# A two-layer decoder trunk on TensorE: x held at another address outside the feed-forward layers, four pairs of sums moved from GpSimd to VectorE, and two wide products ahead of four streams of narrow ones

## The chip, the cores and the metric

The kernel runs on one core of a Trainium2 chip. The metric is the device time of one execution in microseconds (us), and a figure for a kernel is the median of several runs. The engines are named as the profile names them: PE is TensorE (PEld its weight loads), DVE is VectorE, ACT is ScalarE, POOL is GpSimd, SP issues the DMAs.

## The reference

Input and output are 512 tokens of 1024 channels in float32. Layer 0 has native sparse attention (nsa) as its mixer, layer 1 a gated linear recurrence (hgrn); each mixer stands between two feed-forward layers (FFNs) of inner width 2816.

```python
def _swiglu(x, w_gate, w_up, w_down):
    return (jax.nn.silu(x @ w_gate) * (x @ w_up)) @ w_down

    for i in range(DEPTH):                      # DEPTH = 2
        x = _layer_norm(alpha * x + 0.5 * _swiglu(x, ffn1_w_gate[i], ffn1_w_up[i], ffn1_w_down[i]),
                        ln_gain[i, 0], ln_bias[i, 0])
        ...
        y = _nsa(x, ...) if kind == 0 else _hgrn2(x, ...)
        x = _layer_norm(alpha * x + y, ln_gain[i, 1], ln_bias[i, 1])
        x = _layer_norm(alpha * x + 0.5 * _swiglu(x, ffn2_w_gate[i], ffn2_w_up[i], ffn2_w_down[i]),
                        ln_gain[i, 2], ln_bias[i, 2])
```

Both mixers begin with a projection `x @ w_in` and end with one by `w_out`.

## The kernel before

Every float32 operand of a large product is split into a high part (`whi`, `xh`, `xhi`), written by ACT (`split`, L112), and the rest (`wlo`, `xl`, `xlo`), written by DVE (L113). A product is then three products of PE (`mm3`, L128 to L130): high by high, and each high part by the other's rest. In a row such as `ps<-xh,whi` the output stands ahead of the arrow, then the operand that streams through PE (moving), then the one that PEld loads (stationary).

The stages follow one another: FFN 1, nsa, FFN 2 of layer 0, then FFN 1, hgrn, FFN 2 of layer 1. In the profiled execution they begin at about 5, 355, 707, 1051, 1398 and 1745 us. The four FFNs are one function, `ffn_body`. It works on the inner width in two halves, of 12 and 10 blocks of 128, and a group `g` is two such blocks for gate and up together. Group 0 is done by `plain_pair` with products of 256 columns. Every other group is done by `seven`: seven products of half-size blocks (24 PE products of 256 columns each) in place of eight, with sums and differences of the weights formed on DVE (L350, `form`) and of the results on DVE as well (`q2` at L402, `q3` at L404, then L408 to L415). Product 4 of a call that is not `seeded` (groups 1 and 2) needs `q3`. The second half of each FFN consists of five such calls, 840 products. Behind each half stands `down`, products of 512 columns (`ps<-whi,xhi` and its two fellows).

The transposed x is held as `xh` and `xl` in the pool `xt`. In `plain_pair` of group 0, x comes in four blocks of 128 tokens. For blocks 0 and 1 their parts are summed back to float32 (`xb`, L272, a slice of `h`), two instructions of 128 x 1024 on POOL; for blocks 2 and 3 `token_forms` (L173 to L177, DVE) makes the differences between token halves from them, from which the tiles `t0h` to `t2l` are split. Ahead of this stands the layer norm of the stage before (`ln_tok`): statistics and L200, L215, L216 on DVE, and three small POOL instructions L204, L189, L190 between the statistics and L216.

The bytes modulo 256 at which an operand begins in a partition: in the FFNs 224 for `xh`, `xl` and the tiles t0h to t2l, 32 for `whi`, `wlo`, and 32 for both operands of `down`. In the mixers' projections x is at 224 and the weights are at 32, in 96 products at 0. In the mixers x is the moving operand for keys and queries (`ps<-xh,whi`, 480 of them 512 columns wide) and the stationary one where the result has tokens on the partitions (`ps<-whi,xh`, 672 of them 512 wide with weights at 32); 288 more of both kinds are 256 columns wide.

The order on PE is that of the program. On DVE, ACT, POOL and SP a scheduler chooses the order by its own estimates of when each instruction could begin, so that an instruction given to another engine can change the order of its neighbours.

## Time and profile before

| | |
|---|---|
| median of 3 runs | 2110.07 us (2104.12, 2110.07, 2110.17) |
| the profiled execution, and its span | 2099.54 us, 2097.8 us |
| busy: PE, PEld, DVE, ACT, POOL | 98%, 90%, 68%, 47%, 10% |
| mean granted clock of PE | 0.995 |

The profile is of one execution, some 10 us below the median of the runs. Its times within the span are those of the trace. A product's duration in it is modelled; what a stream of products costs is read from the starts, as the distance from one start to the next, which is called the pace here.

### The profile page before, as it was taken

The page shows a single profiled execution, that of the slowest core. Times are in us where ns is not written, and L with a number is a line of the kernel's source. Part 1 is how long each engine was busy: PE and PEld are TensorE (multiplying, and loading weights), DVE is VectorE, ACT ScalarE, POOL GpSimd, SP SyncE. Part 2 cuts the span into 40 slices and gives each one's busy share as a digit, 9 for nine tenths or more (in the row PEclk, how much of TensorE's full clock was granted, in tenths as well). Part 3 has the DMA queues.
Part 4 walks back from the last instruction along what each step waited for, and adds up shares of the span by engine and source line. Part 5 has one row for each costly group of instructions (what it writes and reads, how often), then busy time and mean ns, then how long its engine had stood idle before and what let it go on. Part 6 is the DMA issues. An engine that isn't in the chain of part 4 may idle for free.

```text
span 2097.8 us, 34590 instructions
## 1 busy us (share of the span) xinstructions
PE 2055.2 (98%) x14277; PEld 1885.4 (90%) x14277; DVE 1418.3 (68%) x2124; ACT 976.1 (47%) x1570; POOL 217.2 (10%) x321
## 2 busy tenths in 40 slices
PE   8999999999999999999999999999999999999998
PEld 8998998879898899899899989988788989998996
DVE  8946855377775896486598467664636858955864
ACT  5543552255565354255345335435536734543551
POOL 1000002001122300000110000021321213000002
PEclk9999999999999999999999999999999999999999
DMA  5441342231011145133234412512231023342331
GB/s 181 122 150 51 102 145 76 82 110 41 31 31 51 61 125 157 48 113 115 67 121 124 138 57 86 172 60 90 82 116 31 2 71 101 115 147 61 101 121 41
DMA packets 138762, 194.00 MB, mean 92 GB/s; under 512 B 8571, under 2 KB 117435, under 8 KB 138604
## 3 DMA queue, kind: packets, MB, share of 16 engines
q1 hardware_dynamic: 138604, 191.79, 29.6%
q8 instruction: 112, 1.84, 0.4%
q14 instruction: 46, 0.38, 0.1%
HBM read 189.58 MB, written 2.19 MB: 91 GB/s over the span
## 4 chain that ended last, share of the span: by engine, by line
PE 83%; DVE 10%; POOL 2%; ACT 2%; issue 1%; DMA 1%; DVEq 0%; POOLq 0%; SPq 0%; ACTq 0%
PE ps L128 23%; PE ps L130 23%; PE ps L129 23%; PE po L820 3%; DVE wlo L113 2%; PE ps L804 2%; PE ps L1148 1%; DVE raw L350 1%; PE sc L771 1%; PE sc L772 1%; DVE st L201 1%; DVE x L200 1%; PE ps L543 1%; DVE xl L113 1%; ACT whi L112 1%
## 5 line engine op out<-in xcount | busy, mean ns | idle before, releaser
L113 DVE TENSOR_TENSOR wlo<-raw,whi 128x1024 fp32r<-128x1024 f32 (+1 forms) x253 | 315.2, 1250 | 275.0 <-ACT whi L112 274.3
L112 ACT ACTIVATE whi<-raw 128x1024 fp32r<-128x1024 f32 (+1 forms) x253 | 265.6, 1055 | 359.7 <-PE ps L130 164.5
L128 PE MATMUL ps<-xh,whi 128*128 128x256 f32 (+1 forms) x1120 | 332.9, 297 | 3.0 <-ACT whi L112 1.6
L130 PE MATMUL ps<-xh,wlo 128*128 128x256 f32 (+1 forms) x1120 | 331.1, 296 | 2.3 <-DVE wlo L113 2.3
L129 PE MATMUL ps<-xl,whi 128*128 128x256 f32 (+1 forms) x1120 | 331.0, 296 | 1.2 <-DVE xl L113 1.2
L130 PE MATMUL ps<-whi,xlo 128*128 128x512 f32 x704 | 274.4, 390 | 1.5 <-DVE xlo L113 1.5
L128 PE MATMUL ps<-whi,xhi 128*128 128x512 f32 x704 | 274.4, 390 | 0.0
L129 PE MATMUL ps<-wlo,xhi 128*128 128x512 f32 x704 | 274.0, 389 | 0.0
L130 PEld LDWEIGHTS ps<-xh,wlo 128*128 128x128 f32 x1120 | 212.3, 190 | 10.2 <-DVE wlo L113 2.8
L128 PEld LDWEIGHTS ps<-xh,whi 128*128 128x128 f32 x1120 | 210.8, 188 | 11.8 <-ACT whi L112 2.0
L129 PEld LDWEIGHTS ps<-xl,whi 128*128 128x128 f32 x1120 | 211.0, 188 | 8.9 <-DVE xl L113 1.8
L128 PE MATMUL ps<-xh,xhi 128*128 128x256 f32 x640 | 180.2, 282 | 7.3 <-DVE q L404 7.2
L112 ACT ACTIVATE whi<-fr 128x1024 fp32r<-128x1024 f32 x120 | 126.7, 1059 | 118.6 <-PE ps L129 83.8
L129 PE MATMUL ps<-xl,xhi 128*128 128x256 f32 x640 | 179.8, 281 | 0.0
L130 PE MATMUL ps<-xh,xlo 128*128 128x256 f32 x640 | 179.8, 281 | 0.0
L113 DVE TENSOR_TENSOR wlo<-fr,whi 128x1024 fp32r<-128x1024 f32 x120 | 146.8, 1224 | 47.4 <-ACT whi L112 47.1
L130 PEld LDWEIGHTS ps<-whi,xlo 128*128 128x128 f32 x704 | 132.2, 188 | 30.7 <-DVE xlo L113 3.2
L129 PEld LDWEIGHTS ps<-wlo,xhi 128*128 128x128 f32 x704 | 132.2, 188 | 26.8
L128 PEld LDWEIGHTS ps<-whi,xhi 128*128 128x128 f32 x704 | 132.2, 188 | 26.8
L350 DVE TENSOR_TENSOR raw<-fr 128x1024 f32<-128x1024 f32 x120 | 145.8, 1220 | 13.1 <-DMA fr<-in_ffn_w_up_dram 11.4
L113 DVE TENSOR_TENSOR xlo<-h,xhi 128x1024 fp32r<-128x1024 f32 x44 | 53.9, 1226 | 111.8 <-ACT xhi L112 111.8
L128 PEld LDWEIGHTS ps<-xh,xhi 128*128 128x128 f32 x640 | 121.6, 190 | 8.1 <-DVE q L404 7.8
(267 smaller groups left out, 4737.7 us busy)
## 6 DMA issues: line engine op xcount, KB each, us to landing
raw<-in_ffn_w_down_dram SPq DMA_DIRECT2D x88, 512.0 KB, 3.5
fr<-in_ffn_w_gate_dram SPq DMA_DIRECT2D x80, 512.0 KB, 4.0
fr<-in_ffn_w_up_dram SPq DMA_DIRECT2D x80, 512.0 KB, 5.0
raw<-in_hgrn_w_in_dram SPq DMA_DIRECT2D x32, 512.0 KB, 4.2
raw<-in_nsa_w_in_dram SPq DMA_DIRECT2D x18, 512.0 KB, 3.9
raw<-in_ffn_w_gate_dram SPq DMA_DIRECT2D x8, 512.0 KB, 5.4
raw<-in_ffn_w_up_dram SPq DMA_DIRECT2D x8, 512.0 KB, 4.5
raw<-in_nsa_w_out_dram SPq DMA_DIRECT2D x8, 512.0 KB, 3.4
```

Source lines behind the costliest of these rows:

```text
L112: a = self.nc.scalar.activation(hi, src, AF.Copy)
L113: b = self.nc.vector.tensor_tensor(lo, src, hi.bitcast(F32), op=ALU.subtract)
L128: mm(out, l[0], r[0], start=start, stop=False)
L129: mm(out, l[0], r[1], start=False, stop=False)
L130: mm(out, l[1], r[0], start=False, stop=stop)
L200: nc.vector.scalar_tensor_tensor(x[:, s], x[:, s], float(scale), banks[h], op0=ALU.mult, op1=ALU.add)
L201: nc.vector.bn_stats(st[:, h, :], x[:, s])
L350: tt(out, x, y, op=op)
L543: nc.tensor.matmul(ph, w1[:, j, :], self.ap(z[:, 0:1], 2 * j, [[16, 129]]), start=j == 0, stop=j == 15)
L771: nc.tensor.matmul(sc[:, t - ts[0], :], l, kh[t][g][:, :n], start=True, stop=False)
L804: nc.tensor.transpose(p[:, j * P : j * P + P], pf[:, (b0 + j) * P : (b0 + j + 1) * P], self.ident)
L820: nc.tensor.matmul(po[:, ii, t, :], pt[:, t * (i + 1) + j, :], v[j][:, t, g, :], start=j == 0, stop=j == i)
```

## The change

The tiles of `xh` and `xl` become 64 bytes longer, and `place_xt` sets where x begins in them: at 0 (224 modulo 256, as before) or at 64 bytes (32 modulo 256). In `finish` of the first FFN of each layer x goes to 64 before the first new block is written, in `finish` of the mixer back to 0. So x is at 32 modulo 256 throughout nsa and hgrn, and at 224 in the FFNs. `out_proj` of nsa takes its views of the old x (`ox`) before that. The sums L272 are given to DVE in place of POOL. In the first call of `seven` in an FFN's second half two products of 512 columns, `xh` by `whi`, are put ahead of product 1; their result is overwritten and used by nobody.

```diff
+PLACE = 64
@@ new_xt
-        self.xh = pool.tile([P, 2, NK, 2 * P], F32R, name="xh")
-        self.xl = pool.tile([P, 2, NK, 2 * P], F32R, name="xl")
+        self.xbuf = [pool.tile([P, NK * T + 64], F32R, name=n) for n in ("xh", "xl")]
+        self.place_xt(0)
+
+    def place_xt(self, n):
+        self.xh, self.xl = (b[:, n // 4 : n // 4 + NK * T].rearrange("p (a k t) -> p a k t", a=2, k=NK) for b in self.xbuf)
@@ finish
                 if h == 0 and c >= 2:
+                    self.place_xt(self.place)
                     self.flush(c - 2)
@@ ffn_body
-                                nc.gpsimd.tensor_tensor(xb[:, k], self.xh[:, 0, ks].bitcast(F32), self.xl[:, 0, ks].bitcast(F32), op=ALU.add)
+                                nc.vector.tensor_tensor(xb[:, k], self.xh[:, 0, ks].bitcast(F32), self.xl[:, 0, ks].bitcast(F32), op=ALU.add)
...
-                        self.seven(mid, tf, w3, g, h[:, 2 * pr : 2 * pr + 2, :], g >= NSTD + 2)
+                        self.seven(mid, tf, w3, g, h[:, 2 * pr : 2 * pr + 2, :], g >= NSTD + 2, half == 1 and pr == 0)
@@ seven
+        if first:
+            for _ in range(2):
+                nc.tensor.matmul(b, w[1][0][:, 0, 0, :], self.xr(0)[0], start=True, stop=True, skip_group_check=True)
         product(1, a, True)
@@ out_proj
+        if xh is None:
+            ox = [self.xc(k, c) for k in range(NK) for c in range(NT)]
...
-                l = self.xc(k, c) if xh is None else (xh[k][:, c * P : c * P + P], xl[k][:, c * P : c * P + P])
+                l = ox[NT * k + c] if xh is None else (xh[k][:, c * P : c * P + P], xl[k][:, c * P : c * P + P])
@@ body
-    for r, t.nxt in zip(run, first[1:] + [None]):
+    for r, t.nxt, t.place in zip(run, first[1:] + [None], (PLACE, 0, 0, PLACE, 0, 0)):
```

The change moves instructions on PE, DVE, POOL and, a little, ACT; SP's order of loads is the same in both kernels. The new file has its lines 7 to 12 further down (L113 becomes L120, L200 L207, L204 L211, L216 L223, L272 L280, L330 L338, L350 L358, L402 L414, L404 L416).

The first place is PE's passage from `down` to the second half of an FFN, here the first one. Before:

```order
L128 MATMUL ps<-whi,xhi 128x512
L129 MATMUL ps<-wlo,xhi 128x512
L130 MATMUL ps<-whi,xlo 128x512
L128 MATMUL ps<-xh,whi 128x256
L129 MATMUL ps<-xl,whi 128x256
L130 MATMUL ps<-xh,wlo 128x256
```

In the changed kernel the same passage reads:

```order
L135 MATMUL ps<-whi,xhi 128x512
L136 MATMUL ps<-wlo,xhi 128x512
L137 MATMUL ps<-whi,xlo 128x512
L404 MATMUL ps<-xh,whi 128x512 x2
L135 MATMUL ps<-xh,whi 128x256
L136 MATMUL ps<-xl,whi 128x256
L137 MATMUL ps<-xh,wlo 128x256
```

The two products stand between the last wide product of `down` and the first narrow one; on PE nothing else has moved anywhere.

The second place is the head of FFN 1 of layer 1, where the layer norm of token block 3 (x_74) meets the sums. DVE before, from the splits of blocks ahead to the second step of the norm:

```order
L113 TENSOR_TENSOR xl<-ps,xh 128x4x128 x2
L201 BN_STATS st<-x_74 128x6
L200 SCALAR_TENSOR_TENSOR x_74<-x_74,ps 128x512
L201 BN_STATS st<-x_74 128x6
L202 BN_AGGR mv<-st 128x2
L215 SCALAR_TENSOR_TENSOR x_74<-x_74,mv,lng 128x512 x2
L216 SCALAR_TENSOR_TENSOR x_74<-x_74,ry,lnb 128x512 x2
```

POOL before, at the same place:

```order
L212 TENSOR_TENSOR x_73<-x_73,lng 128x512
L213 TENSOR_TENSOR x_73<-x_73,lnb 128x512
L272 TENSOR_TENSOR h<-xh,xl 128x1024 x2
L204 TENSOR_SCALAR lm<-mv 128x1
L189 TENSOR_SCALAR ry<-mv 128x1
L190 TENSOR_TENSOR ry<-ry,mhalf 128x1
```

DVE in the changed kernel:

```order
L120 TENSOR_TENSOR xl<-ps,xh 128x4x128 x2
L208 BN_STATS st<-x_74 128x6
L207 SCALAR_TENSOR_TENSOR x_74<-x_74,ps 128x512
L280 TENSOR_TENSOR h<-xh,xl 128x1024
L208 BN_STATS st<-x_74 128x6
L280 TENSOR_TENSOR h<-xh,xl 128x1024
L209 BN_AGGR mv<-st 128x2
L222 SCALAR_TENSOR_TENSOR x_74<-x_74,mv,lng 128x512 x2
L223 SCALAR_TENSOR_TENSOR x_74<-x_74,ry,lnb 128x512 x2
```

The two sums stand ahead of the norm's statistics `mv` on DVE now, and on POOL nothing stands any more between L220 (before: L213) and L211 (before: L204). In FFN 2 of both layers the two L280 rows stand right behind the two L223 rows of block 3, ahead of the split `xl` of block 2; in the first FFN of all they stand behind the first three splits `wlo<-raw,whi`.

The third place is DVE's way to `q3` of group 1, here in FFN 2 of layer 0. Before:

```order
L113 TENSOR_TENSOR wlo<-fr,whi 128x1024
L113 TENSOR_TENSOR xlo<-raw,xhi 128x1024
L330 TENSOR_TENSOR h<-ps,sg 128x512
L113 TENSOR_TENSOR xl<-h,xh 128x1024
L113 TENSOR_TENSOR wlo<-fr,whi 128x1024
L113 TENSOR_TENSOR wlo<-raw,whi 128x1024
L113 TENSOR_TENSOR wlo<-fr,whi 128x1024
L350 TENSOR_TENSOR raw<-fr 128x1024 x2
L113 TENSOR_TENSOR wlo<-raw,whi 128x1024
L402 TENSOR_TENSOR q_7785<-ps,p_7784 128x512
L350 TENSOR_TENSOR fr<-fr,raw 128x8x128
L404 TENSOR_TENSOR q_7865<-ps,q_7785 128x512
```

In the changed kernel:

```order
L120 TENSOR_TENSOR wlo<-fr,whi 128x1024
L338 TENSOR_TENSOR h<-ps,sg 128x512
L120 TENSOR_TENSOR xl<-h,xh 128x1024
L120 TENSOR_TENSOR wlo<-fr,whi 128x1024
L120 TENSOR_TENSOR wlo<-raw,whi 128x1024
L358 TENSOR_TENSOR raw<-fr 128x1024
L120 TENSOR_TENSOR wlo<-fr,whi 128x1024
L358 TENSOR_TENSOR raw<-fr 128x1024
L120 TENSOR_TENSOR xlo<-raw,xhi 128x1024
L414 TENSOR_TENSOR q_7787<-ps,p_7786 128x512
L120 TENSOR_TENSOR wlo<-raw,whi 128x1024
L416 TENSOR_TENSOR q_7867<-ps,q_7787 128x512
```

Counted from the first L173 (now L180) of block 2, 20 instructions of 128 x 1024 elements stand ahead of L404 before, and 18 ahead of L416 now: one `form` raw<-fr and the `form` fr<-fr,raw have moved behind it. The same holds for the FFNs of layer 1.

## Rows read from the trace of the kernel before

**Rows 1.** The page: the span, the busy time of each engine with its share of the span and its instructions, and the chain that ended last, by engine.

```profile
span 2097.8 us, 34590 instructions
...
PE 2055.2 (98%) x14277; PEld 1885.4 (90%) x14277; DVE 1418.3 (68%) x2124; ACT 976.1 (47%) x1570; POOL 217.2 (10%) x321
...
PE 83%; DVE 10%; POOL 2%; ACT 2%; issue 1%; DMA 1%; DVEq 0%; POOLq 0%; SPq 0%; ACTq 0%
```

**Rows 2.** The timeline of PE in the first FFN: start, duration, engine, line, operation and tiles. The first and the last of 91 rows in its first half, then the first and the last of 87 rows in its second half.

```profile
59.78 0.28 PE L129 MATMUL ps<-t2l,whi 128*128 128x256 f32 x1
...
69.98 0.28 PE L129 MATMUL ps<-t0l,whi 128*128 128x256 f32 x1
...
249.76 0.28 PE L129 MATMUL ps<-xl,whi 128*128 128x256 f32 x1
...
259.89 0.28 PE L128 MATMUL ps<-xh,whi 128*128 128x256 f32 x1
```

**Rows 3.** Busy time by windows, PE alone: the window, its length, busy us (and products), granted clock, share and GB/s of the DMA engines. The first row lies in the first half of FFN 1 of layer 0, the next to last in that of FFN 2 of layer 1; the others lie in the second halves of the four FFNs. Products that run over a window's edge count in it.

```profile
83.00:133.00 50.00, 50.00 (x443) 1.00 0.54 164
...
245.00:295.00 50.00, 50.00 (x427) 1.00 0.31 95
...
900.00:950.00 50.00, 50.00 (x427) 1.00 0.33 97
...
1245.00:1295.00 50.00, 50.00 (x427) 1.00 0.29 90
1800.00:1850.00 50.00, 50.00 (x443) 1.00 0.39 121
1940.00:1990.00 50.00, 50.00 (x427) 1.00 0.34 104
```

**Rows 4.** The timeline of PE, streams of 512 columns: the first and the last of 46 rows of `down`, of 46 rows of hgrn with x stationary, and of 45 rows of hgrn with x moving.

```profile
159.68 0.39 PE L128 MATMUL ps<-whi,xhi 128*128 128x512 f32 x1
...
169.88 0.39 PE L128 MATMUL ps<-whi,xhi 128*128 128x512 f32 x1
...
1519.68 0.39 PE L130 MATMUL ps<-whi,xl 128*128 128x512 f32 x1
...
1529.98 0.39 PE L130 MATMUL ps<-whi,xl 128*128 128x512 f32 x1
...
1559.62 0.39 PE L129 MATMUL ps<-xl,whi 128*128 128x512 f32 x1
...
1569.89 0.39 PE L128 MATMUL ps<-xh,whi 128*128 128x512 f32 x1
```

**Rows 5.** The timeline of PE at two passages into streams of 256 columns: from `down` into the second half of the first FFN, and behind a wait of PE at the head of FFN 2 of layer 0. In brackets: idle time ahead of the row and what ended it.

```profile
198.89 0.39 PE L130 MATMUL ps<-whi,xlo 128*128 128x512 f32 x1
199.12 0.28 PE L128 MATMUL ps<-xh,whi 128*128 128x256 f32 x1
199.24 0.28 PE L129 MATMUL ps<-xl,whi 128*128 128x256 f32 x1
...
720.68 0.39 PE L129 MATMUL ps<-xl,whi 128*128 128x256 f32 x1 [0.48 <-DVE xl L113]
720.90 0.28 PE L130 MATMUL ps<-xh,wlo 128*128 128x256 f32 x1
```

**Rows 6.** The timelines of POOL and DVE at the heads of three FFNs: first FFN, FFN 2 of layer 0, FFN 1 of layer 1.

```profile
8.84 5.68 POOL L272 TENSOR_TENSOR h<-xh,xl 128x1024 f32<-128x1024 f32 x2 [7.55 <-DVE xl L113]
...
9.87 6.87 DVE L113 TENSOR_TENSOR wlo<-raw,whi 128x1024 fp32r<-128x1024 f32 x3 [0.25 <-ACT whi L112]
...
712.99 4.75 POOL L272 TENSOR_TENSOR h<-xh,xl 128x1024 f32<-128x1024 f32 x2 [1.62 <-DVE x L216]
...
715.41 0.69 DVE L173 TENSOR_TENSOR h<-ps,h 128x512 f32<-128x512 f32 x1 [1.99 <-POOL h L272]
...
1052.62 5.21 POOL L272 TENSOR_TENSOR h<-xh,xl 128x1024 f32<-128x1024 f32 x2
1057.81 0.66 POOL L204 TENSOR_SCALAR lm<-mv 128x1 f32<-128x1 f32 x1
...
1053.95 4.44 DVE L215 SCALAR_TENSOR_TENSOR x<-x,mv,lng 128x512 f32<-128x512 f32 x2
1059.33 1.41 DVE L216 SCALAR_TENSOR_TENSOR x<-x,ry,lnb 128x512 f32<-128x512 f32 x2 [0.95 <-POOL ry L190]
```

**Rows 7.** The timelines of PE and DVE at the waits of PE near the heads of the FFNs: first FFN, FFN 2 of layer 0, FFN 1 of layer 1 (three rows of PE and DVE, and its wait for the norm), FFN 2 of layer 1.

```profile
12.34 0.58 PE L130 MATMUL ps<-xh,wlo 128*128 128x256 f32 x1 [1.96 <-DVE wlo L113]
...
747.84 0.38 PE L128 MATMUL ps<-xh,xhi 128*128 128x256 f32 x1 [2.50 <-DVE q L404]
...
1060.14 0.55 PE L159 MATMUL ps<-ident,x 128*128 128x128 f32 x3 [1.60 <-DVE x L216]
...
1091.60 1.22 DVE L350 TENSOR_TENSOR fr<-fr,raw 128x1024 f32<-128x1024 f32 x1
1092.73 0.68 DVE L404 TENSOR_TENSOR q<-ps,q 128x512 f32<-128x512 f32 x1
...
1093.47 0.39 PE L128 MATMUL ps<-xh,xhi 128*128 128x256 f32 x1 [2.00 <-DVE q L404]
...
1786.52 0.39 PE L128 MATMUL ps<-xh,xhi 128*128 128x256 f32 x1 [2.69 <-DVE q L404]
```

**Rows 8.** Busy time by windows behind the waits for L404: the window, its length, then busy us (and instructions) of PE, PEld, DVE, ACT and POOL, granted clock, share and GB/s of the DMA engines.

```profile
1091.40:1098.40 7.00, 5.00 (x30) 4.93 (x30) 7.00 (x9) 3.36 (x4) 0.00 (x0) 0.76 0.16 34
...
1786.60:1793.60 7.00, 7.00 (x48) 7.00 (x49) 7.00 (x9) 4.01 (x5) 0.00 (x0) 0.76 0.49 146
...
747.00:754.00 7.00, 6.06 (x50) 5.86 (x51) 7.00 (x10) 4.14 (x5) 0.00 (x0) 1.00 0.33 99
```

More of the change, by code (lines that the diff above doesn't have):

```diff
@@ L330, in plain_pair, with seven @@
             nc.vector.tensor_tensor(h[:, fc, :], banks[2 + fc], sg, op=ALU.mult)
-    def seven(self, pool, tf, w3, g, h, seeded):
+    def seven(self, pool, tf, w3, g, h, seeded, first):
         nc = self.nc
```

## The prediction

> **What bounds the kernel now.** I read the page first: PE is busy for 2055 of 2098 us and carries 83% of the chain that ended last, DVE 10%, POOL 2% [rows 1]. So the time is PE's products times their pace, plus some 40 us in which it is idle; only what changes a pace or a wait of PE counts. A "busy" PE is no PE at its best, however, so next I read starts. Products of 256 columns run at two paces: (69.98 - 59.78) / 90 = 113.3 ns in the first half of the first FFN, (259.89 - 249.76) / 86 = 117.8 ns in its second [rows 2], with the same operands at the same addresses. The windows tell that this is no accident of one place: 443 products fit in 50 us of first halves, 427 in 50 us of each of the four second halves, with the granted clock at 1.00 in all [rows 3]. Products of 512 columns have a pace that goes with the address: 10.20 / 45 = 226.7 ns in `down` (both operands at 32 modulo 256), 10.30 / 45 = 228.9 with x stationary at 224, 10.27 / 44 = 233.4 with x moving at 224 [rows 4]. Last I read who ends PE's waits at the heads of the FFNs: DVE, in every row [rows 7], and there DVE itself had been held by POOL [rows 6].
>
> **Part 1, x at 32 in the mixers.** The 480 wide products with x moving get both operands at 32, as in `down`: 480 x (233.4 - 226.7) = 3.2 us less. The 672 with x stationary: 672 x (228.9 - 226.7) = 1.5 us. For the 96 with weights at 0 and for those of 256 and fewer columns no row has the new pair of addresses; the nearest are the two paces of [rows 2], so 288 products of 256 columns move by 0 to 4.5 ns either way, up to 1.3 us. I take 0 there. A little of this may be lost where attention is waiting for something else: I take -4.6 us, between 0 and -6. `place_xt` and `ox` are only views; the three orders of the mixers are as before, so they cost nothing.
>
> **Part 2, the sums on DVE.** On POOL a pair took 5.68, 4.75 and 5.21 us [rows 6]. On DVE an instruction of this size stands 1092.73 - 1091.60 = 1.13 us ahead of the next [rows 7], so a pair adds 2.3 us to DVE's queue. What hides it: DVE sat 1.99 us waiting for POOL's sums at 715.41, and beside them its own work was slow: three `wlo` took 6.87 us where 3.5 is three of 1.13 and a tail, two L215 took 4.44 where the two L216 took 1.41 [rows 6]. Without that cover it would be 2.3 us later for all that is queued behind it, the splits `xl` of block 2 and the token forms first. Head by head:
>
> First FFN: PE waited 1.96 us for the first `wlo` [rows 7]. That was 2.29 of 6.87; alone it takes about 1.2, so the wait shrinks by 1.1: -1.1 us (0 to -1.5, as a second such wait may go too). The sums come behind these splits.
>
> FFN 2 of layer 0: the sums go where DVE's idle 1.99 us was, and behind them DVE is about where it was (a slow `wlo` beside POOL less, 2.3 of work more: 0.2 us earlier). But ahead of L404 stand 18 instructions of 1.13 us in place of 20, so it ends 0.2 + 2 x 1.13 = 2.5 us earlier. PE waited 2.50 us for it [rows 7]; it also arrives up to 0.5 earlier, as its wait of 0.48 for `xl` [rows 5] goes. PE's time behind that wait is set by L404 alone: -2.5 us, and about half a microsecond of wait stays.
>
> FFN 1 of layer 1: here POOL's sums stand ahead of L204, which begins at 1057.81 though `mv` was ready before L215 began at 1053.95. With the sums on DVE ahead of `mv` it is ready at about 1056.1; L204 to L190 take 1059.3 - 1057.8 = 1.5, so L216 begins at 1057.6, not 1059.33 [rows 6]. The wait of 1.60 of the transposes shrinks by 1.5. L216 to L404 was 33.4 us without a gap; now 1057.6 + 33.4 - 2.3 = 1088.7, end 1089.4. PE arrives at 1091.5 - 1.5 = 1090.0. So the wait of 2.00 goes as well, and with it what followed: in the window behind it the granted clock was 0.76, and 30 products took 5.00 us, 1.6 more than at 113.3 ns [rows 8]. Sum -5.1 us.
>
> FFN 2 of layer 1: like that of layer 0, -2.5, of a wait of 2.69. The window behind had clock 0.76, 48 products in 7.00 us, again 1.6 us lost [rows 8]; behind the wait of 2.50 in layer 0 it stayed at 1.00. I take it that a short wait leaves it at 1.00: -4.1.
>
> Together -12.8 us. Bounds: -5 if the clock still falls and the queue gains only part, -15 if all waits named go.
>
> **Part 3, two wide products ahead of each second half.** They cost 8 x 0.233 = 1.9 us by [rows 4]. What can they give? No row shows a wide product of x at 224 directly ahead of narrow ones. Passing from `down`, the narrow stream is at 117.8 from its first step, 199.12 to 199.24, and stays there for all 840 products [rows 2, 3, 5]. Behind a wait, the first step is 0.22 us, as wide as a wide product, and the stream ends in the fast pace of first halves [rows 3, 5]. So the pace is decided at the entrance, and the two products change the entrance: they have the narrow products' addresses and come with their slower step (233.4 in place of 226.7), which shifts PEld against PE. The bounds are 0 and 4 x 840 x (117.8 - 113.3) = 15.1 us. Between them there is nothing, as a stream is in one pace or the other; the nearest rows, entrances that are not from `down`, lie on the fast side, so I take -15.1 + 1.9 = -13.2 us.
>
> The Trainium skill's page "TensorE: Matmul & The Clock Gate" (Part 2, Step-by-step: what each phase is for) speaks against parts 1 and 3: streaming and weight loads have two independent read ports, so a load takes nothing from the running product. By that rule the sum would be -10.9 us. The trace does not agree: one kind of product has three paces by address [rows 4].
>
> **Sum.** -4.6 - 12.8 - 13.2 = -30.6 us. Against the profiled execution: 2099.5 - 30.6 = 2069. It lies 10.5 us below the median of the runs, so for the median I say 2110 - 30.6 = 2079.5, about 2080 us.
>
> **Rivals.**
> The entrance stays slow (no flip): part 3 costs 1.9 and gives nothing. For it: the passage from wide to narrow in [rows 5] and the counts of all second halves in [rows 3] are slow, and a wide product is what stands ahead of them. Against: those had other addresses. -4.6 - 12.8 + 1.9 = -15.5, 2095 us. Two halves of four would be 2087.
>
> Addresses and entrances do nothing: the spread in [rows 4] comes from the shape of the streams around, not from bytes, and only the sums help: -12.8 + 1.9 = -10.9, 2099 us. Against it: `down` and both hgrn streams are as wide and as dense as each other.
>
> The sums gain nothing: DVE's gain is eaten by the 2.3 us that it does more, the waits for L404 stay as they are, and no entrance flips: -4.6 + 1.9 = -2.7, 2107 us, which is no change that can be measured.
>
> Slower: DVE is full from the head to L404. If the work moved behind L404 is not late but needed sooner, each L404 comes 2.3 us later. Then 4 x 2.3 = 9.2 us, and 1.6 for a clock that falls in FFN 2 of layer 0 too, so +10.8; the other parts without a flip give -2.7: +8.1, 2118 us. It decides itself at 715.41: if DVE's idle time there was not POOL's sums but something that arrives as late as before, this is the case. For it: L216 to L404 has no gap. Against it: the order, and the 1.99 us named for POOL [rows 6].
>
> **How the numbers follow.** Forecast 0.48 (own range 2073 to 2088), no flip 0.30, addresses do nothing 0.09, no gain from the sums 0.08, slower 0.05. A difference under 0.3%, 6.3 us, can about not be told from none here, as the three runs spread over 6 us. The first three cases are faster: 0.87; the fourth is the same: 0.08; the last slower: 0.05. The range takes in the first three with their bounds: from 2080 less 8 (sums at -15, mixers at -6, the runs' spread) to 2099 and 5 for it, so 2072 to 2104.
>
> **What would show it.** Part 1: `ps<-xh,whi` of 512 columns at 226.7 ns in nsa and hgrn, `ps<-whi,xh` too. Part 2: no L272 on POOL; three `wlo` in about 3.5 us in the first FFN; the waits for L404 at 0.5 us or below, none of 2 us, and the clock at 1.00 behind them. L216 of block 3 in FFN 1 of layer 1 1.5 us or more earlier against the stage's begin. Part 3: windows of 50 us in second halves with 443 products. The prediction is wrong if these windows still have 427, if first halves, which now lose their waits, fall from 443 to 427 (4 to 5 us each), or if the waits for L404 grow.

## The result, and the profile after

The changed kernel takes 2086.35 us (median of 5 runs, 2084.49 to 2092.30) against 2106.63 of the kernel before (5 runs, 2100.88 to 2110.17): 0.9907 of it, with an interval of 0.989 to 0.9924. That is 20 us less, two thirds of the forecast 30.6; the time lies inside the range. The two profiled executions are only 15.1 us apart, 2097.8 and 2082.7 us of span. The execution profiled before lies 7 us under the median of its runs; how much of that the traces show is said below.

The page of the changed kernel, the lines that answer to [rows 1]:

```profile
span 2082.7 us, 34594 instructions
...
PE 2044.8 (98%) x14285; PEld 1878.1 (90%) x14285; DVE 1418.6 (68%) x2132; ACT 974.1 (47%) x1570; POOL 196.8 (9%) x313
```

POOL lost its 20 us of sums, DVE's busy time did not grow (its instructions beside POOL had been slow), and PE has eight products more.

Busy time of PE by windows of 50 us in the changed kernel, as in [rows 3]: one window in a first half, then one in each of the four second halves.

```profile
83.00:133.00 50.00, 50.00 (x427) 1.00 0.51 158
...
245.00:295.00 50.00, 50.00 (x444) 1.00 0.33 99
900.00:950.00 50.00, 50.00 (x444) 1.00 0.34 106
1245.00:1295.00 50.00, 50.00 (x443) 1.00 0.34 106
1940.00:1990.00 50.00, 50.00 (x443) 1.00 0.32 106
```

All second halves hold 443 or 444 products now, where 427 stood before. The window in the first FFN's first half went the other way, from 443 to 427.

PE's waits in the changed kernel: who waits for whom, us in total, times, longest.

```profile
PE ps L135 <- DVE c L420: 5.1, 6, 2.3
...
PE ps L135 <- DVE q L416: 2.2, 3, 1.1
```

and the row of the kernel before with which they compare:

```profile
PE ps L128 <- DVE q L404: 7.2, 3, 2.7
```

The wait for `q3` shrank from 7.2 to 2.2 us, as forecast, and a wait for `c`, the next result that PE needs of DVE, stands beside it with 5.1. Together it is 7.3 us, where it was 7.2. Most of the new 5.1 us are two waits: 2.34 us at the head of FFN 1 of layer 1, shown below, and 1.46 us in the first FFN, where PE had no wait for `q3` before:

```profile
54.08 0.36 PE L135 MATMUL ps<-xh,xhi 128*128 128x256 f32 x1 [1.46 <-DVE c L420]
```

A ledger from the starts of PE's products says where the 15.1 us of the two traces lie. I took the begin of each `down` and the first start behind it, so that each stretch is a difference of two starts, in us:

| stretch | before | changed | difference |
|---|---|---|---|
| four second halves, each | 98.93 | 95.68 | 4 x -3.25 |
| start to first `down` (first FFN) | 133.8 | 136.1 | +2.3 |
| nsa, and the first half of FFN 2 | 475.9 | 475.6 | -0.2 |
| first half of FFN 1, layer 1 | 125.0 | 123.1 | -1.9 |
| hgrn, and the first half of FFN 2 | 472.0 | 469.6 | -2.4 |
| all stretches of `down` | 495.4 | 495.6 | +0.2 |

So the second halves alone gave 13 us, and all the rest, of which 17 were expected, gave 2.

### The profile page after: what moved, and what is told of

Read it like the earlier page. It is cut to its first block, busy times and chain, and to the rows that moved or that the text cites. A ratio compares the mean times of both kernels' runs of the same rounds, so it can differ in the third digit from the quotient of the medians.

```text
span 2082.7 us, 34594 instructions
## 1 busy us (share of the span) xinstructions
PE 2044.8 (98%) x14285; PEld 1878.1 (90%) x14285; DVE 1418.6 (68%) x2132; ACT 974.1 (47%) x1570; POOL 196.8 (9%) x313
## 4 chain that ended last, share of the span: by engine, by line
PE 82%; DVE 11%; ACT 3%; POOL 2%; DMA 2%; issue 1%; SPq 0%; DVEq 0%; POOLq 0%; ACTq 0%
PE ps L135 23%; PE ps L137 23%; PE ps L136 23%; PE po L832 3%; DVE wlo L120 2%; PE ps L816 2%; PE ps L1163 1%; DVE raw L358 1%; PE sc L784 1%; PE sc L783 1%; DMA fr<-in_ffn_w_up_dram 1%; ACT whi L119 1%; DVE st L208 1%; PE ps L555 1%; DVE xl L120 1%
## 5 line engine op out<-in xcount | busy, mean ns | idle before, releaser
L120 DVE TENSOR_TENSOR wlo<-raw,whi 128x1024 fp32r<-128x1024 f32 (+1 forms) x253 | 311.8, 1237 | 269.1 <-ACT whi L119 268.3
L120 DVE TENSOR_TENSOR wlo<-fr,whi 128x1024 fp32r<-128x1024 f32 x120 | 146.3, 1220 | 42.3 <-ACT whi L119 42.3
L358 DVE TENSOR_TENSOR raw<-fr 128x1024 f32<-128x1024 f32 x120 | 145.6, 1220 | 16.1 <-DMA fr<-in_ffn_w_up_dram 14.7
L120 DVE TENSOR_TENSOR xlo<-h,xhi 128x1024 fp32r<-128x1024 f32 x44 | 53.9, 1226 | 111.4 <-ACT xhi L119 111.4
```

The source lines that it names most:

```text
L120: b = self.nc.vector.tensor_tensor(lo, src, hi.bitcast(F32), op=ALU.subtract)
L358: tt(out, x, y, op=op)
```

## The experiments

Each kernel but the repetition changes one or two things: the first is made from the kernel before, all others from the changed kernel. "Held" means that the sums of weights wait for `c` on DVE, as told below. Times are medians. The ratio is to runs of the kernel before, taken beside each set of kernels on the same chip (medians 2105.91, 2107.08 and 2106.81 us).

| kernel | time | ratio to before, interval |
|---|---|---|
| wide pair alone | 2093.47 | 0.9932, 0.9914 to 0.9949 |
| without the wide pair | 2099.41 | 0.9962, 0.9946 to 0.9979 |
| sums back on POOL | 2086.77 | 0.9908, 0.989 to 0.9926 |
| x at 224 everywhere | 2090.62 | 0.9922, 0.9902 to 0.9941 |
| one wide product | 2089.18 | one run |
| two wide products at 32 | 2100.56 | one run |
| x at 32 everywhere | 2101.43 | one run |
| forms held behind c | 2078.08 | 0.9858, 0.9833 to 0.9882 |
| the changed kernel again | 2086.86 | 0.99, 0.9879 to 0.9921 |
| held, sums on POOL | 2079.68 | 0.9869, 0.9851 to 0.9887 |
| held, one wide product in each half | 2077.38 | 0.986, 0.9845 to 0.9874 |
| held, x at 224 everywhere | 2076.86 | 0.9862, 0.9845 to 0.9879 |

The kernel with x at 32 everywhere is left out of the next table, since its paces mix. From each other trace I worked out a second table, with the starts of all narrow products of the four first halves: what a step has over 113.3 ns is put down to the slow pace (steps of 116 to 119 ns, summed with the few at its entrance), to a low clock (200 to 217 ns) or to a wait (over 240 ns). "hgrn" is the time from the first start behind FFN 1's last `down` to FFN 2's first product, "nsa" the same in layer 0. All in us.

| kernel | each second half | four first halves | slow pace | low clock | waits | nsa | hgrn |
|---|---|---|---|---|---|---|---|
| before | 98.93 | 502.2 | 0.9 | 4.9 | 13.7 | 352.3 | 347.6 |
| changed | 95.68 | 501.3 | 7.0 | 2.5 | 10.7 | 351.3 | 347.2 |
| changed, again | 95.68 | 501.5 | 7.7 | 2.4 | 9.5 | 354.8 | 347.0 |
| wide pair alone | 95.68 | 505.3 | 5.9 | 3.3 | 13.6 | 355.4 | 348.5 |
| without the pair | 98.93 | 504.1 | 9.4 | 4.8 | 8.7 | 351.5 | 346.1 |
| sums on POOL | 95.68 | 508.6 | 10.2 | 3.9 | 12.0 | 352.5 | 346.0 |
| x at 224 everywhere | 95.68 | 506.6 | 9.9 | 3.7 | 11.7 | 354.2 | 349.6 |
| one wide product | 95.44 | 503.3 | 9.0 | 3.2 | 9.6 | 356.2 | 346.1 |
| two wide at 32 | 99.39 | 501.3 | 5.3 | 3.9 | 10.3 | 354.3 | 345.5 |
| held | 95.68 | 492.7 | 2.9 | 2.4 | 6.1 | 354.1 | 346.4 |
| held, sums on POOL | 95.68 | 496.4 | 2.9 | 2.7 | 8.2 | 352.6 | 347.0 |
| held, one in each half | 95.44 | 494.3 | 9.7 | 2.4 | 1.1 | 351.1 | 347.4 |
| held, x at 224 | 95.68 | 491.0 | 2.9 | 2.3 | 4.2 | 357.8 | 348.4 |

### The parts alone and taken back

The wide pair alone, put into the kernel before:

```diff
+        if first:
+            for _ in range(2):
+                nc.tensor.matmul(b, w[1][0][:, 0, 0, :], self.xr(0)[0], start=True, stop=True, skip_group_check=True)
         product(1, a, True)
```

> The kernel before with nothing but the two wide products ahead of each second half. Theory A (the wide pair decides the pace of a second half by itself): all four second halves at 113.3 ns (443 or 444 products in 50 us, 95.7 us from their begin to the second down in place of 98.9), 13 us less than before, ratio about 0.994. Rival C (the second halves became fast because the sums or x's place changed what ran beside them): second halves stay at 117.8 ns and 98.9 us, and the two products cost 1.9 us, ratio about 1.001.

Measured: 12.4 us less by the medians, 95.68 us in each second half. Theory A holds, rival C is out. A second thing shows in its trace. Up to the first wide product at 201 us the program is that of the kernel before, instruction for instruction on PE, and yet this window holds 427 products, where [rows 3] has 443:

```profile
83.00:133.00 50.00, 50.00 (x427) 1.00 0.50 158
```

So a first half can be slow before anything of the change has run on PE.

The changed kernel without the pair:

```diff
-            for _ in range(2):
-                nc.tensor.matmul(b, w[1][0][:, 0, 0, :], self.xr(0)[0], start=True, stop=True, skip_group_check=True)
```

> The changed kernel without the wide products: x at 32 in the mixers and the sums on VectorE alone. Theory A: second halves at 117.8 ns again, 98.9 us each, so 13 us more than the changed kernel; against the kernel before only some 2 us less (ratio about 0.999). Rival C: second halves stay at 113.3 ns, ratio to before about 0.992. Rival D (the forecast of the sums holds on the whole and one execution's first halves were bad luck): ratio about 0.992 too, but with second halves at 117.8 ns and first halves at 113.3.

Measured: ratio 0.9962 to before, 13 us over the changed kernel, second halves at 98.93 us. Its first window in a second half holds 427 products again, as in [rows 3], and the other three hold 426 or 427:

```profile
245.00:295.00 50.00, 50.00 (x427) 1.00 0.29 89
```

Theory A's size of 2 us for the other two parts together was too small, rival D's 16 too large: they give 6.5 by the medians, 8 by the ratio (4 to 11 by its interval).

The sums back on POOL:

```diff
-                                nc.vector.tensor_tensor(xb[:, k], ...)
+                                nc.gpsimd.tensor_tensor(xb[:, k], ...)
```

> The changed kernel with the sums back on GpSimd. Theory A (what VectorE gains at the heads is given back by new waits for c one step later and by first halves that fall to 117.8 ns): waits of 2.0 to 2.7 us for q3 are back at three heads, the waits for c in front of product 4's successors are gone, first halves hold 443 products in 50 us; 1 us more than the changed kernel, between -3 and +3. Rival D: 12.8 us more than the changed kernel, ratio to before about 0.996 in place of 0.991.

Measured: 2086.77 us, 0.4 more than the changed kernel, inside the noise of both. The waits for `q3` are back at two of the three heads (5.2 us in all), those for `c` are 0.2. The moved sums by themselves are worth nothing that the times can show. First halves are not all fast, as Theory A had it: three of the four were slow, in whole or in part, in this execution.

x at 224 everywhere:

```diff
-PLACE = 64
+PLACE = 0
```

> The changed kernel with x at 224 modulo 256 everywhere (PLACE = 0). Theory A: wide products of the mixers at 233.3 ns (x moving) and 228.9 ns (x stationary) again in place of 227.0 and 226.7, narrow ones at 113.4 or 117.8 ns in place of 119.9; in time only 1 to 1.5 us more than the changed kernel, as hgrn's waits for ScalarE and attention's for VectorE take up most of it. Rival (the forecast's term): 4.6 us more.

Measured: 2090.62, 4.3 us more than the changed kernel, near the forecast's term; but the two intervals overlap for most of their width, so the size stays open here; the last kernel below tries it again.

### What makes a second half fast

```diff
-            for _ in range(2):
+            for _ in range(1):
```

> The changed kernel with one wide product ahead of each second half in place of two. Theory A1 (what counts is that the last step ahead of the narrow stream is one of x at 224, 233 ns in place of 227): one is enough, all four second halves at 113.3 ns (95.4 us to the second down). Rival A2 (it takes two steps until the weight loads stand otherwise): second halves at 117.8 ns, 98.9 us, 13 us more.

Measured: 95.44 us in each second half, 0.24 less than with two. One is enough.

```diff
-                nc.tensor.matmul(b, w[1][0][:, 0, 0, :], self.xr(0)[0], ...)
+                nc.tensor.matmul(b, w[1][0][:, 0, 0, :], w[1][0].rearrange("p m k j -> p (m k j)")[:, :512], ...)
```

> The changed kernel, but the two products stream the 512 columns of a weight tile at 32 modulo 256 in place of x at 224; both operands are then at 32 as in down. Theory A1 (the address makes the slower step, and that makes the entrance): their steps are 227 ns and second halves stay at 117.8 ns, 98.9 us, some 13 us more than the changed kernel. Rival A3 (any two products that are not of down, with another output bank and one weight tile, do it): second halves at 113.3 ns.

Measured: 99.39 us in each second half. Two useless wide products with both operands at 32 cost their 0.45 us and change nothing. The entrances side by side, on the timeline of PE; first the changed kernel, where the pair takes from 201.43 to 201.89, 233 ns each:

```profile
201.20 0.39 PE L137 MATMUL ps<-whi,xlo 128*128 128x512 f32 x1
201.43 0.63 PE L404 MATMUL ps<-xh,whi 128*128 128x512 f32 x2
201.89 0.28 PE L135 MATMUL ps<-xh,whi 128*128 128x256 f32 x1
202.01 0.28 PE L136 MATMUL ps<-xl,whi 128*128 128x256 f32 x1
202.13 0.28 PE L137 MATMUL ps<-xh,wlo 128*128 128x256 f32 x1
202.25 0.28 PE L135 MATMUL ps<-xh,whi 128*128 128x256 f32 x1
```

then the kernel with the pair at 32, where the pair takes from 201.42 to 201.87, 227 ns each:

```profile
201.42 0.61 PE L404 MATMUL ps<-whi 128*128 128x512 f32 x2
201.87 0.28 PE L135 MATMUL ps<-xh,whi 128*128 128x256 f32 x1
201.99 0.28 PE L136 MATMUL ps<-xl,whi 128*128 128x256 f32 x1
```

In the first the steps run in from 122 ns to 113 within four products; in the second they are 118 from the first one on, as in [rows 5].

The address was tried the other way round too, with x at 32 in the FFNs:

```diff
-        self.place_xt(0)
+        self.place_xt(PLACE)
-    for r, t.nxt, t.place in zip(run, first[1:] + [None], (PLACE, 0, 0, PLACE, 0, 0)):
+    for r, t.nxt, t.place in zip(run, first[1:] + [None], (PLACE,) * 6):
```

> The changed kernel with x at 32 modulo 256 in the FFNs too (the tiles t0h to t2l stay at 224). Reading of the trace of the changed kernel: products of 256 columns with both operands at 32 run at 119.9 ns in the mixers. If that goes with the address, every product of 256 columns of xh and xl in the FFNs runs at 119 to 120 ns in both halves, those of t0h to t2l between them at 113 to 118; a second half takes 99 to 100 us, and the kernel 25 to 35 us more than the changed one. If 119.9 is a matter of the mixers, FFNs stay at 113.3 and 117.8 ns and the time is that of the changed kernel.

Measured: 2101.43 us, about 15 more than the changed kernel and not 25 to 35. The pace goes with the operand. On the timeline of PE, the last product of a `t1` tile (at 224) and the first of x (at 32), some left out:

```profile
229.95 0.28 PE L137 MATMUL ps<-t1h,wlo 128*128 128x256 f32 x1
230.06 0.28 PE L135 MATMUL ps<-xh,whi 128*128 128x256 f32 x1
...
231.00 0.28 PE L137 MATMUL ps<-xh,wlo 128*128 128x256 f32 x1
231.12 0.28 PE L135 MATMUL ps<-xh,whi 128*128 128x256 f32 x1
```

Up to 230.06 the steps are 110 to 120 ns by these rounded starts, 113 to 114 on the mean of the tile; behind it 119 to 120. The expectation was too high since the products of the tiles t0 to t2, three sevenths of all, went at 113 to 115 in both halves: coming from x at 32, a stream at 224 was fast every time.

### Where the gain of the sums went

On DVE's timeline of the changed kernel, at group 1 of FFN 1 in layer 1, from `q3` to `c`; the last row is PE's:

```profile
1084.61 0.68 DVE L416 TENSOR_TENSOR q<-ps,q 128x512 f32<-128x512 f32 x1
1086.34 1.23 DVE L358 TENSOR_TENSOR raw<-fr 128x1024 f32<-128x1024 f32 x1 [1.05 <-DMA fr<-in_ffn_w_up_dram]
1087.48 0.42 DVE L398 TENSOR_TENSOR h<-ps,sg 128x256 f32<-128x256 f32 x1
1087.82 1.22 DVE L358 TENSOR_TENSOR fr<-fr,raw 128x1024 f32<-128x1024 f32 x1
1089.07 1.22 DVE L358 TENSOR_TENSOR raw<-fr 128x1024 f32<-128x1024 f32 x1
1090.21 0.68 DVE L420 TENSOR_TENSOR c<-ps,q 128x512 f32<-128x512 f32 x1
...
1091.04 0.36 PE L135 MATMUL ps<-xh,xhi 128*128 128x256 f32 x1 [2.34 <-DVE c L420]
```

Counted from the begin of the stage (the first start behind the `down` ahead of it, 1051.8 us before and 1047.6 now), `q3` begins 3.9 us earlier than in [rows 7], where the forecast had 4.0. But the forms that moved behind it are now between it and `c`: three of them, the first waiting 1.05 us for its own data. L416 to L420 takes 5.6 us, while PE needs `c` one product (24 steps, 2.7 us) behind `q3`. To test it, the forms of the group behind were held:

```diff
         def form(x, y, op, out=None):
...
-            tt(out, x, y, op=op)
+            with self.after(self.held):
+                tt(out, x, y, op=op)
...
-        tt(c[:, 1], e.rearrange(two, m=2), ...)
+        ins = tt(c[:, 1], e.rearrange(two, m=2), ...)
+        self.held = [] if seeded else [ins]
```

> The changed kernel with one thing held back: the sums of weights (form) of the group behind one that is not seeded may not be issued on VectorE ahead of that group's first c. Theory A (forms moved behind q3 now stand ahead of c, and wait for their DMA there): the waits of TensorE for c, 5.1 us in the changed kernel's trace, fall below 1 us, those for q3 stay near 2.2 us; 4 to 5 us less than the changed kernel in the waits, in the time 2 to 5 less as first halves differ from run to run by their pace. Rival (VectorE is full, and what is held back is missing one step later): waits for wlo of the next group of 1 to 2 us come in their place, time within 1.5 us.

Measured: 2078.08 us, ratio 0.9858, some 9 us less than the changed kernel. In its waits `q3`, which Theory A had left at 2.2 us, does not appear at all, `c` has 0.7 us, and a wait for ACT has grown in their place:

```profile
PE ps L135 <- ACT ps L411: 3.1, 4, 0.8
...
PE ps L135 <- DVE c L421: 0.7, 2, 0.4
```

On DVE's timeline at the same place `c` now stands right behind `q3` and waits for PE, no longer PE for it:

```profile
1079.01 0.69 DVE L417 TENSOR_TENSOR q<-ps,q 128x512 f32<-128x512 f32 x1
1080.19 0.42 DVE L399 TENSOR_TENSOR h<-ps,sg 128x256 f32<-128x256 f32 x1 [0.50 <-ACT sg L398]
1082.50 0.69 DVE L421 TENSOR_TENSOR c<-ps,q 128x512 f32<-128x512 f32 x1 [1.88 <-PE ps L137]
```

Theory A holds in kind; its size of 2 to 5 us was too small. The gain is larger than the 5.1 us of waits: by the second table first halves fell by 8.6 us against the first trace of the changed kernel, of which 4.6 are waits and 4.1 slow pace. Each short wait in a first half is an entrance at which the narrow stream may fall to 117.8 ns; that the slow pace shrank because there were fewer waits is argued and not shown by itself, but the three kernels with held forms and no added product all have 2.9 us of it.

Is it then the sums' new place at all, or the order that came with it?

```diff
-                                nc.vector.tensor_tensor(xb[:, k], ...)
+                                nc.gpsimd.tensor_tensor(xb[:, k], ...)
```

> The kernel c_first with the sums back on GpSimd: forms held behind c, but no sums on VectorE. By its order 16 instructions of 128 x 1024 stand ahead of q3 from the first token form on, 20 in the kernel before and 18 in the changed one. Theory A (the queue ahead of q3 and c is what counts, not who does the sums): waits for q3 and c are below 1 us in all; only what the sums on GpSimd cost directly is back (1.1 us for wlo in the first FFN, 1.2 for the norm in the third, 0.5 for xl in the second), so 2 to 3 us more than c_first. Rival (the sums' place is what frees VectorE): waits of 2 to 2.7 us for q3 are back, 6 to 9 us more than c_first.

Measured: 2079.68 us. No wait for `q3` is left here either, and 0.3 us for `c`; what is back are 2.5 us for `wlo` (0.8 in the changed kernel) and 1.6 for the norm (0.4). First halves are 3.7 us longer than with the sums on DVE, the times 1.6 apart, which their intervals do not tell from none. So the order of DVE's queue ahead of `q3` and `c` is worth 7 us with the sums on POOL and 8 to 9 with the sums on DVE; the sums' place itself is worth 0 to 4.

The changed kernel once more:

> The changed kernel once more, unaltered, on the chip of the three kernels beside it. If the pace of first halves (113.3 or 117.8 ns) is settled anew in each execution by the waits in it, other first halves are slow than in the first trace, with the same orders and second halves at 95.7 us in all four FFNs; time within 0.3% of 2086 us. If it goes with the program, the same first halves are slow: the first FFN, the second from its group 2 on, and a piece of the fourth.

Measured: 2086.86 us, the same orders, all second halves at 95.68 us. In FFN 2 of layer 0 the window from 785 to 825 us has another pace than in the first trace. First trace, then the repetition:

```profile
785.00:825.00 40.00, 40.00 (x342) 1.00 0.58 175
```

```profile
785.00:825.00 40.00, 40.00 (x355) 1.00 0.56 176
```

The pace of a first half is settled anew in each execution, at its waits: in no trace does a narrow stream with x at 224 go from one pace to the other without an interruption. This goes some way to tell why the profile of before lay 7 us under the median of its runs. With 0.9 us it has the least slow pace of all traces; the others without held forms have 5.3 to 10.2. The trace of the wide pair alone, the same program but for the pair, has first halves 3.1 us longer and mixers 4.0 us longer than it. A second trace of the kernel before was not taken.

### The two last ones

```diff
-                        self.seven(..., half == 1 and pr == 0)
+                        self.seven(..., (half == 1 and pr == 0) or g == NSTD + 2)
...
-            for _ in range(2):
+            for _ in range(1):
```

> The kernel c_first with one wide product in place of two ahead of each second half and one more in each first half ahead of group 3's product 1. Each costs 0.23 us, so 1.9 us in all as before. Theory A: second halves 95.4 us; the last three groups of each first half always at 113.3 ns, which takes back the part of the slow pace that falls there (0 to 2.3 us an FFN, 2.5 us in c_first's trace); 0 to 4 us less than c_first. Rival (a wide product ahead of a stream that is not behind down does not set the pace): first halves fall to 117.8 ns as before, time of c_first.

Measured: 2077.38 us, that of the kernel with held forms. The second halves are at 95.44 us, but in the first halves Theory A falls: all four went from 113.3 to 117.8 ns at the added product and stayed there, the slow pace is 9.7 us. On PE's timeline, first the added product in the first half, then the one behind `down`:

```profile
74.22 0.39 PE L405 MATMUL ps<-xh,whi 128*128 128x512 f32 x1
74.45 0.28 PE L135 MATMUL ps<-xh,whi 128*128 128x256 f32 x1
74.57 0.28 PE L136 MATMUL ps<-xl,whi 128*128 128x256 f32 x1
...
199.11 0.39 PE L405 MATMUL ps<-xh,whi 128*128 128x512 f32 x1
199.34 0.28 PE L135 MATMUL ps<-xh,whi 128*128 128x256 f32 x1
199.47 0.28 PE L136 MATMUL ps<-xl,whi 128*128 128x256 f32 x1
```

It is the same product with the same addresses. Behind a fast narrow stream its step is 226 ns and the next ones are 118; behind `down` its step is 233 ns and the next ones run in to 113.3. So the product by itself does not make a stream fast; what stood ahead of it counts too. Its step alone is not the rule either. At the end of both mixers the last wide product passes without a gap into the first 24 narrow products of FFN 2, after a step of 231 to 235 ns, and in all 13 traces with x at 224 in the FFNs these went at 117.8 ns, some behind a run-in of three steps: 26 entrances of 26. In FFN 2 of layer 0 the kernel before had it already, with a step of 0.23 us and then (709.86 - 707.15) / 23 = 117.8 ns; the first and the last of 24 narrow rows behind the wide one:

```profile
706.92 0.39 PE L130 MATMUL ps<-whi,xl 128*128 128x512 f32 x1
707.15 0.28 PE L128 MATMUL ps<-xh,whi 128*128 128x256 f32 x1
...
709.86 0.28 PE L130 MATMUL ps<-xh,wlo 128*128 128x256 f32 x1
```

There a weight streams and not x. What makes an entrance fast is not shown beyond these cases.

```diff
-PLACE = 64
+PLACE = 0
```

(in the kernel with held forms)

> The kernel c_first with x at 224 modulo 256 everywhere. Theory A: wide products of the mixers at 233.3 and 228.9 ns again; hgrn 2 to 3 us longer (348 to 350 us in place of 346), nsa 0 to 2 us longer within a scatter of 5, so 2 to 5 us more than c_first. Rival (the mixers' own waits take up all of it): within 1.5 us of c_first.

Measured: 2076.86 us, 1.2 less than with x at 32, at intervals of some 4 and 5 us either way: the medians fit the rival, but do not rule out the lower end of Theory A. In its trace, of an execution of 2081.73 us, hgrn is 2.0 us longer, nsa 3.7. In the whole second table hgrn takes 347.6 to 349.6 us with x at 224 (four traces, 348.5 on average) and 345.5 to 347.4 with x at 32 (nine traces, 346.5): about 2 us, and the two do not overlap. nsa scatters from 351.1 to 357.8 over all of them, and its share is not settled. In the times x at 32 gave 4.3 us in one pair of kernels and lost 1.2 in the other; what it is worth stays open.

## Why the prediction was right or wrong

**Wide products: right in size, the reason only in part.** Forecast 13.2 us less, measured 13.0 in the traces (4 x 3.25) and 12.4 in the time of the pair alone. Every one of the 40 second halves behind one or two wide products of x at 224 was fast, every one of the 12 of the kernels without them, or with the two products at 32, was slow (the kernel with x at 32 everywhere left aside, since its paces mix). That the pace is decided at the entrance is borne out, and so is that PEld stands otherwise to PE: in the fast pace a weight load begins 110 ns ahead of its product, in the slow one 114 to 115, in the traces before and after. The reason given, the slower step, fits the product that took 226 ns and made things worse, but not the 26 entrances from the mixers, which had a step of 231 to 235 ns and stayed slow. Two of those stood in the trace of before, so the remark that entrances not from `down` lie on the fast side was wrong there; and in most other traces 5 to 10 us of first halves were slow. That all four second halves flipped was forecast on a reason that is not enough, and so was luck in part.

**x at 32: the new paces right, one old pace and the sum open.** In the changed kernel the wide products with x moving take (1560.00 - 1549.80) / 45 = 226.7 ns and those with x stationary (1449.79 - 1439.82) / 44 = 226.6, as forecast from `down`. The first and the last of 45 and of 46 rows of PE's timeline:

```profile
1439.82 0.39 PE L136 MATMUL ps<-wlo,xh 128*128 128x512 f32 x1
...
1449.79 0.39 PE L135 MATMUL ps<-whi,xh 128*128 128x512 f32 x1
...
1549.80 0.39 PE L137 MATMUL ps<-xh,wlo 128*128 128x512 f32 x1
...
1560.00 0.39 PE L137 MATMUL ps<-xh,wlo 128*128 128x512 f32 x1
```

The narrow ones, taken at 0, have a third pace of (367.90 - 363.82) / 34 = 120.0 ns, against 113.4 or 117.8 before; 288 of them cost 0.6 to 1.9 us of the gain. The first and the last of 35 rows:

```profile
363.82 0.28 PE L136 MATMUL ps<-xl,whi 128*128 128x256 f32 x1
...
367.90 0.28 PE L137 MATMUL ps<-xh,wlo 128*128 128x256 f32 x1
```

The term for x stationary was taken from one trace. Before, all of hgrn's 576 such products went at 228.9 ns; in the three other traces with x at 224 the first 384 of them went at 233.3, here (1450.21 - 1439.71) / 45, the first and the last of 46 rows with x at 224 everywhere:

```profile
1439.71 0.40 PE L136 MATMUL ps<-wlo,xh 128*128 128x512 f32 x1
...
1450.21 0.40 PE L136 MATMUL ps<-wlo,xh 128*128 128x512 f32 x1
```

So a wide stream has two paces at one pair of addresses too, and counted from 233.3 the term is 384 x 6.6 + 288 x 2.2 = 3.2 us in place of 1.5. What the traces show of 4.6 is about 2 in hgrn and an unsettled rest in nsa.

**The sums: this step failed.** Forecast 12.8 us less; the first halves, which hold all of it, took 502.2, 505.3 and 508.6 us in the three traces with sums on POOL, and 501.3 to 506.6 in the six with sums on DVE, neither with held forms: 2 us on average. The single waits moved nearly as worked out: `wlo` in the first FFN from 2.3 to 0.8, the norm from 1.6 to 0.4 (its L223 begins 1.2 us earlier against the stage's begin, where 1.5 or more was forecast), `q3` from 7.2 to 2.2. The granted clock stayed at 1.00 behind them in both traces of the changed kernel (low clock 4.9 to 2.5 and 2.4), but it fell behind a wait for `c` of 2.26 us without the pair and of 2.41 us with x at 224 everywhere. What was wrong is the sentence "PE's time behind that wait is set by L404 alone". The two forms that the order showed behind L404 were booked as gone. They stand ahead of `c` (L408, now L420), which PE needs one product further; at the head of FFN 1 of layer 1 a third one and a wait for data stand there with them. What is late next was asked for `q3` alone. The first FFN, booked with 1.1 us less, got a new wait for `c` of 1.46. On the averages of those nine traces waits fell by 3.0 us, where 9.6 were booked, and the low clock by 0.6, where 3.2 were; the slow pace, booked at nothing, rose by 2.4, less than it scatters. The rival that DVE is full and the gain is eaten was in the text with 0.08; it was the nearest to this part, though it had the waits for `q3` stay as they were.

**The slow pace of first halves** was named as a thing that would make the prediction wrong, and it cost 7 us in the changed kernel's trace. That it is a cost of the change is not shown: kernels of both kinds have it, 0.9 to 10.2 us with the sums on POOL and 5.3 to 9.9 with them on DVE, where no forms are held. The forecast took its baseline of 443 products from the one trace that was nearly free of it.

**The rule on read ports.** The Trainium skill's page "TensorE: Matmul & The Clock Gate" (Part 2, Step-by-step: what each phase is for), by which a weight load takes nothing from the running product, stands in the prediction as a reason against parts 1 and 3. The traces do not agree that addresses do nothing: with nothing changed but what the two wide products stream, a weight tile at 32 or x at 224, their steps are 227 or 233 ns and a second half takes 99.4 or 95.7 us. Whether a weight load is what takes the time is not shown.

**The sum** came out at 20 of 30.6 us: 13 from the pair, and 4 to 11 by the interval of the kernel without it from x's place and the sums together, which the runs do not divide further than said above. The kernel with held forms is at 2078.08 us, near the forecast 2079.5, but that does not bear the forecast out: with the sums back on POOL it takes 2079.68, so what it gained beyond the changed kernel came from the order of DVE's queue and not from the sums' place.

## What to carry to other kernels

When an instruction that an engine waits for is made earlier by moving others behind it, follow the queue to the next result that the same engine needs: what was moved stands there now, and holding it behind that result as well gave 7 to 9 us here, where the first move alone gave 2 in the first halves and nothing that the times could show. Where a stream of products has two paces, look at the starts at its entrance, try one cheap product there, and count on it only where the same stream stands ahead of it each time. A baseline of one trace can be a lucky one: compare its waits and paces with a second execution before a gain is booked against it.

## What the runs showed of the hardware

A stream of 256 column products with x at 224 and weights at 32 modulo 256 keeps one of two paces, 113.3 or 117.8 ns, until it is interrupted, in all of the traces here. Where wide products of x at 224 stood behind `down`, their step was 233 ns and the stream went at 113.3 (40 of 40 second halves); where the last wide step was 225 to 227 ns it went at 117.8; behind the last wide product of a mixer, with 231 to 235 ns, it went at 117.8 too (26 of 26); behind waits either occurred. 512 column products with x stationary at 224 have two paces as well, 228.9 and 233.3 ns. With both operands at 32 the order of things is turned round: wide products are at their best (226.7 against 233.4 ns), narrow ones at their worst (120 ns). Why is not shown. Behind PE's wait of 2.34 us in the changed kernel the granted clock stayed at 1.00, the higher of its two levels (2.4 GHz). Behind the same wait with x at 224 everywhere, 2.41 us, the window has 0.76, so a part of it at the lower level (1.2 GHz), and so it was before behind waits of 2.00 and 2.69 us but not behind one of 2.50 [rows 8]. The length of the wait does not tell the two apart. The windows of the first two, in the columns of [rows 8]:

```profile
1091.00:1098.00 7.00, 6.96 (x61) 6.99 (x62) 7.00 (x9) 5.39 (x8) 0.00 (x0) 1.00 0.48 151
...
1091.50:1098.50 7.00, 6.86 (x45) 6.89 (x46) 6.83 (x9) 4.13 (x6) 0.00 (x0) 0.76 0.46 150
```
